# Block sums accumulated in PSUM, and the modulation product in rows of 512 with other intervals, in a two-layer diffusion backbone on one core

## The chip, the cores and the metric

The kernel runs on one core of a Trainium2 chip, as one launch. The metric is device time in microseconds (us). The engines are named as in the profile: PE (TensorE, matmuls), PEld (its weight loads), DVE (VectorE), ACT (ScalarE), POOL (GpSimd) and SP (which here only issues DMAs). Each engine works through its own list of instructions in order; semaphores hold an instruction back until what it needs is there.

## The reference, cut to what matters

The trunk has two layers over 256 context and 512 latent tokens of 1024 channels. Each layer is a half-step FFN, a token mixer (attention and gating in layer 0, a recurrence in layer 1) and a second half-step FFN. Every one of these steps is modulated by vectors that come from a product of the conditioning vector with `ada_w`:

```
mx = split(silu(c)     @ ada_w[l] + ada_b[l], 9)      # latent tokens
mc = split(silu(c_ctx) @ ada_w[l] + ada_b[l], 9)      # context tokens
h  = rmsnorm(x, g) * (1 + scale) + shift
x  = x + 0.5 * gate * ((silu(h @ wg) * (h @ wu)) @ wd) # 1024 -> 2816 -> 1024
```

Everything is float32.

## The kernel before, in words

A float32 product is made of three passes in the PE's fast format: `mm3` (lines 118 to 123) multiplies high part by high part, high by low and low by high. ACT makes the high part of an operand by a rounding copy, DVE the low part by a subtraction (`split`, line 125).

Three of the four FFNs, (layer 0, first), (layer 0, second) and (layer 1, first), save matmuls: the pairs of gate or up columns after the first pair go through `seven` (line 747), which makes a product of 2 by 2 blocks out of seven block products instead of eight. A call covers 256 columns of weights and both halves L and R (384 tokens each) of the activations; a block product is 12 matmuls of 384 columns, so a call is 84. `seven` runs 20 times per FFN, 60 times in all; it is called once for the gate (its results go to a SiLU on ACT) and once for the up weights (its results are multiplied with the SiLU by DVE and split for the down product). I call the block products M1 to M7 by their keys. Before the change they run in the order 7, 1, 6, 5, 2, 4, 3 into four PSUM banks; M2 is added to M1's bank, M4 to M7's and M3 to M5's. The remaining sums are made on DVE with an intermediate `u` = M6 - M1, which ACT starts by copying M1 out of PSUM (lines 763 to 778). The combined weight blocks for the seven products are prepared by the class `Seven` (line 202): per call four sums and seven low parts on DVE, seven high parts on ACT.

An FFN goes through groups of four column pairs' halves: four calls of `seven` (336 matmuls), then a down stage of 192 matmuls whose results ACT scales and POOL adds to a copy of x in device memory by an accumulating DMA (`down`, lines 673 to 686).

PSUM has eight banks. Before the change all of them are one pool, handed out in turn by `bank` (line 105).

The modulation (`ada_jobs`, lines 460 to 503) streams `ada_w` through SBUF in 128 chunks of 512 KB with two buffers. DVE multiplies each row of a chunk with the conditioning value of its partition and adds it up (lines 485 and 487), and per four row blocks transposes and reduces the result. This is background work: a counter of planned PE time (`clk`) runs `ada_event` (line 512), which issues one step, an instruction or two, every 500 or 800 ns of that planned time; `mod(l, m)` (line 518) issues all that is left of a vector at once when it is needed. It pauses at the end of each FFN until the next norm is done, and in the mixer of layer 0. The framework's scheduler then sets the final order of each engine's list from these issues.

Of the kernel before, what the change touches and what calls it, by code (L numbers as in the profile page):

```python
# [12 lines left out]
F32 = mybir.dt.float32  # L13
# [76 lines left out]
def hybrid_kernel(ctx: ExitStack, tc: tile.TileContext, a: dict, out: bass.AP):  # L90
# [9 lines left out]
    tp = ctx.enter_context(tc.tile_pool(name="tp", bufs=8))  # L100
    psp = ctx.enter_context(tc.tile_pool(name="psp", bufs=8, space=PSUM))
    dp = ctx.enter_context(tc.tile_pool(name="dp", bufs=1, space=DRAM))


    def bank(name="ps"):
        return psp.tile([128, 512], F32, tag="ps", name=name)

# [94 lines left out]
    class Seven(Chunk):  # L202
# [5 lines left out]
        def prep(self):  # L208
# [14 lines left out]
            before = None  # L223
            for key in (7, 1, 6, 5, 2, 4, 3):
# [183 lines left out]
    for i in range(3, 6):  # L408
# [6 lines left out]

    ada_halves = [(j, h) for j in [(0, m, cc) for m in (2, 4, 3, 5, 7, 6, 8) for cc in range(4)]
                  + [(1, m, cc) for m in (1, 0, 2, 4, 3, 5, 7, 6, 8) for cc in range(4)] for h in range(2)]
    ada_tiles, ada_seen = {}, set()

    def ada_load(i):  # L420
        if i < len(ada_halves) and i not in ada_seen:
            (l, m, cc), h = ada_halves[i]
            w = adap.tile([128, 4, 256], F32, tag="aw", name="aw")
            sp.dma_start(out=w, in_=a["ada_w"][l, h * 512:h * 512 + 512, m * 1024 + cc * 256:m * 1024 + cc * 256 + 256]
                         .rearrange("(k p) c -> p k c", p=128))
            ada_tiles[i] = w
            ada_seen.add(i)
# [32 lines left out]
    def ada_jobs():  # L460
# [14 lines left out]
        for i, ((l, m, cc), h) in enumerate(ada_halves):  # L475
# [3 lines left out]
            if h == 0:  # L479
                acc = adap.tile([128, 2, 256], F32, tag="acc", name="acc")  # L480
            for k in range(4):
                for v in range(nv):
                    s = cs[:, h * 4 + k, v:v + 1]
                    if h == 0 and k == 0:
                        dve.tensor_scalar(acc[:, v, :], w[:, k, :], s, None, op0=ALU.mult)
                    else:
                        dve.scalar_tensor_tensor(acc[:, v, :], w[:, k, :], s, acc[:, v, :], op0=ALU.mult, op1=ALU.add)  # L487
                    yield
                if k == 3 and late:
                    late.pop(0)()  # L490
            if h == 1:
                if cc == 0:
                    red = adap.tile([128, 4, nv, 8], F32, tag=f"red{nv}", name="red", bufs=1)
                t = adap.tile([128, 512], F32, tag="acc", name="acc_t")[:, 0:nv * 256]
                dve.transpose(t, acc[:, 0:nv].rearrange("p v c -> p (v c)"))
                yield
                dve.tensor_reduce(red[:, cc], t.rearrange("p (v j r) -> p v j r", v=nv, r=32), axis=mybir.AxisListType.X, op=ALU.add)
                yield
                if cc == 3:
                    late.append(lambda l=l, m=m, nv=nv, red=red: finish(l, m, nv, red))  # L500
# [4 lines left out]
    ada = ada_jobs()  # L505
    bg = {"on": True, "hold": False, "over": False}

# [132 lines left out]
    def ffn(l, j, halves, before, nxt, reserve=(), pre={}):  # L640
# [7 lines left out]
        with tc.tile_pool(name=f"ffn{l}{j}", bufs=4) as fp:  # L648
# [88 lines left out]
            def operand(key, k):  # L737
# [7 lines left out]
                return hi[kk][:, c], lo[kk][:, c]  # L745

            def seven(ch, emit):

                ps = {n: bank("pgu")[:, 0:384] for n in (7, 1, 6, 5)}
                u, v, w = (temp("uvw")[:, 0:384] for _ in range(3))  # L750
                for key, to in ((7, 7), (1, 1), (6, 6), (5, 5), (2, 1), (4, 7), (3, 5)):
                    need(ch, key)
# [6 lines left out]
                    for k in range(4):  # L759
                        mm3(ps[to], (h[:, k], lw[:, k]), operand(key, k), k == 0 and key == to, k == 3, again=key != to)  # L760
                    stream["used"] -= 1
                    pump()
                    if key == 1:
                        act.copy(u, ps[1])
                    elif key == 6:
                        dve.tensor_tensor(u, ps[6], u, op=ALU.subtract)
                        dve.tensor_tensor(v, ps[7], u, op=ALU.add)  # L767
                    elif key == 5:
                        dve.tensor_tensor(v, v, ps[5], op=ALU.subtract)
                        emit(1, R, v)  # L770
                    elif key == 2:
                        emit(0, L, ps[1])
                    elif key == 4:
                        dve.tensor_tensor(w, ps[7], u, op=ALU.add)
                        emit(1, L, w)
                    elif key == 3:
                        dve.tensor_tensor(u, ps[5], u, op=ALU.subtract)
                        emit(0, R, u)

            def gate_up_seven(p, G):  # L780
                s = {}

                def gate(f, c, src):
                    t = s[f, c.start] = temp("silu")[:, 0:384] if (f, c) == (0, L) else src
                    act.activation(t, src, AF.Silu)
# [12 lines left out]
            for gi, (f0, ng, dn) in enumerate(steps):  # L798
                G = {f: (fp.tile([128, NT], F32R, tag="ghi", name="ghi"), fp.tile([128, NT], F32R, tag="glo", name="glo"))
                     for f in range(f0, f0 + ng)}  # L800
                if gi < len(steps) - 1:
                    for p in range(f0, f0 + ng, 2):
                        if saving and p:
                            gate_up_seven(p, G)
                            continue
# [9 lines left out]
                if saving:  # L815
                    gate_up_seven(f0, G)
                    gate_up_seven(f0 + 2, G)
                    for i in range(2):
                        X[i] = xp.tile([128, 4, NT], F32, tag="x", name=f"x{i}")
# [605 lines left out]
    for cc in range(4):  # L1425
# [4 lines left out]
        if cc == 0:  # L1430
            two = arrive(*TB)
            for key in pre:
                pre[key] = bank("pre")
        for k in ks:
# [19 lines left out]
    norms = ffn(0, 0, halves, [], norm_of(0, 1), {"ahead": 1}, pre)  # L1454
    bg.update(on=True, hold=True)
    even_mixer(norms)
    norms = project_out(cwo0, halves, gates(0, 5, 1.0), norm_of(0, 2))
    bg["hold"] = False
    norms = ffn(0, 1, halves, norms, norm_of(1, 0))
# [82 lines left out]
```

## Time and profile before

| | us |
|---|---|
| median of 3 runs | 2670.96 (2668.26 to 2675.2) |
| the profiled execution | 2671.05 |
| its span | 2669.3 |
| PE busy | 2554.3 (96%) |
| PEld busy | 2367.2 (89%) |
| DVE busy | 2023.6 (76%) |
| ACT busy | 1197.1 (45%) |

The profile is one execution. Matmuls are pipelined, so a busy PE is not a PE at its full rate: the number of matmuls in a stretch tells more than the busy time. Times in the rows are microseconds from the start of the span. In this profile the first FFN lies between about 60 and 640 us, the mixer of layer 0 until about 950, the second FFN until about 1490, the third until about 2040; then come the recurrence and the last FFN, which the change does not touch.

### The profile page before, as it was taken

Reading aid. Unit: us, or ns where it says so; the run is one execution under the profiler, and the core shown is the slowest. Engines: PE = TensorE matmul, PEld = TensorE weight load, DVE = VectorE, ACT = ScalarE, POOL = GpSimd, SP = SyncE. Lnnn points to the kernel's source line nnn. Section 1 sums busy time; section 2 is a strip of 40 time slices with the busy share of each in tenths; the row PEclk is TensorE's granted clock in tenths of the full one; section 3 lists DMA queues with packets and bytes.
Section 4 is the critical chain, followed back from the end, with each engine's and each line's share of the span. In section 5 each row is a group of like instructions: output and inputs, shape, how many; then the busy total and the mean of one; then the engine's idle time right before and its main releaser. Section 6 shows DMA issues by size and latency. Waiting matters only on the chain.

```text
span 2669.3 us, 38325 instructions
## 1 busy us (share of the span) xinstructions
PE 2554.3 (96%) x14340; PEld 2367.2 (89%) x14340; DVE 2023.6 (76%) x4252; ACT 1197.1 (45%) x2325; POOL 240.8 (9%) x389
## 2 busy tenths in 40 slices
PE   7799999999999999999999998999999999999998
PEld 4689999898899998999989898999899988888887
DVE  7989989898757699999978887557467898644444
ACT  3344434444655344443444443344444997433322
POOL 0021121200000002112120010210210000000000
PEclk9899999999999999999999898999999999999999
DMA  9275575763110417556675255553553213233221
GB/s 318 64 181 139 151 170 144 183 179 122 32 33 11 149 63 175 137 154 164 163 187 185 92 142 150 96 116 91 112 128 122 64 60 114 82 102 101 95 95 56
DMA packets 281202, 328.49 MB, mean 123 GB/s; under 512 B 19984, under 2 KB 238264, under 8 KB 280504
## 3 DMA queue, kind: packets, MB, share of 16 engines
q1 hardware_dynamic: 246032, 278.69, 32.9%
q0 software_dynamic: 34560, 47.20, 11.6%
q8 instruction: 112, 1.84, 0.3%
q14 instruction: 74, 0.61, 0.1%
q10 hardware_dynamic: 424, 0.15, 0.0%
HBM read 262.04 MB, written 63.96 MB: 122 GB/s over the span
## 4 chain that ended last, share of the span: by engine, by line
PE 70%; DVE 17%; DMA 5%; ACT 4%; issue 2%; POOL 1%; SPq 0%; ACTq 0%; DVEq 0%; POOLq 0%
PE pgu L112 33%; PE pd L112 20%; PE ps L112 9%; PE po L112 4%; DMA aw<-in_ada_w_dram 4%; DVE acc L487 4%; DVE w L219 3%; PE pv L112 1%; DVE w L192 1%; PE sl L112 1%; PE pt L1080 1%; PE sc L112 1%; DVE hlo L598 1%; ACT w L189 1%; DVE glo L127 1%
## 5 line engine op out<-in xcount | busy, mean ns | idle before, releaser
L112 PE MATMUL pgu<-hhi,w 128*128 128x384 f32 (+2 forms) x3008 | 830.3, 350 | 33.7 <-DVE uvw L767 14.7
L112 PE MATMUL pd<-ghi,w 128*128 128x256 f32 (+2 forms) x2528 | 651.6, 345 | 9.4 <-ACT ghi L126 9.2
L112 PEld LDWEIGHTS pgu<-hhi,w 128*128 128x128 f32 x3008 | 556.7, 191 | 65.6 <-DVE uvw L767 17.1
L112 PE MATMUL pgu<-hlo,w 128*128 128x384 f32 (+2 forms) x1504 | 524.4, 349 | 1.9 <-DVE hlo L598 1.4
L112 PEld LDWEIGHTS pd<-ghi,w 128*128 128x128 f32 x2528 | 444.7, 190 | 63.3 <-ACT ghi L126 13.8
L112 PE MATMUL pd<-glo,w 128*128 128x512 f32 (+2 forms) x1264 | 435.0, 346 | 1.9 <-DVE glo L127 1.9
L112 PE MATMUL pgu<-form,w 128*128 128x384 f32 x2160 | 405.0, 338 | 9.1 <-ACT form L126 6.8
L112 PEld LDWEIGHTS pgu<-form,w 128*128 128x128 f32 x2160 | 379.7, 189 | 14.1 <-ACT form L126 7.4
L487 DVE SCALAR_TENSOR_TENSOR acc<-aw,cs,acc 128x256 f32<-128x256 f32 x784 | 343.9, 481 | 38.2 <-DMA aw<-in_ada_w_dram 36.5
L189 ACT ACTIVATE w<-raw 128x512 fp32r<-128x512 f32 x396 | 241.0, 627 | 202.6 <-PE pgu L112 79.9
L192 DVE TENSOR_TENSOR w<-raw,w 128x512 fp32r<-128x512 f32 x396 | 267.8, 688 | 76.3 <-ACT w L189 74.1
L684 POOL DMA_DIRECT2D kept<-add x240 | 208.9, 948 | 1188.7 <-ACT add L683 1176.3
L219 DVE TENSOR_TENSOR w<-raw,w 128x512 fp32r<-128x512 f32 x360 | 239.5, 686 | 94.4 <-ACT w L236 93.8
L112 PEld LDWEIGHTS pgu<-hlo,w 128*128 128x128 f32 x1504 | 288.1, 192 | 15.9 <-DVE hlo L598 2.3
L236 ACT ACTIVATE w<-raw 128x512 fp32r<-128x512 f32 x360 | 213.9, 625 | 185.4 <-DVE raw L233 89.3
L112 PEld LDWEIGHTS pd<-glo,w 128*128 128x128 f32 x1264 | 240.8, 191 | 29.9 <-DVE glo L127 5.3
L683 ACT ACTIVATE add<-pd,gate 128x256 f32<-128x256 f32 x240 | 136.9, 579 | 202.4 <-PE pd L112 177.7
L112 PE MATMUL ps<-hhi,w 128*128 128x384 f32 (+1 forms) x704 | 197.6, 355 | 4.8 <-ACT t L1296 3.4
L112 PEld LDWEIGHTS ps<-hhi,w 128*128 128x128 f32 x704 | 132.5, 194 | 11.8 <-ACT t L1296 4.1
L112 PE MATMUL ps<-hlo,w 128*128 128x384 f32 (+1 forms) x352 | 124.7, 354 | 3.3 <-DVE hlo L598 3.2
L112 PE MATMUL po<-hhi,w 128*128 128x384 f32 (+1 forms) x512 | 114.3, 313 | 2.5 <-ACT hhi L126 2.5
L637 DVE SCALAR_TENSOR_TENSOR x<-pd,gate,x 128x256 f32<-128x256 f32 (+3 forms) x128 | 69.9, 564 | 52.6 <-PE pd L112 51.9
(293 smaller groups left out, 3072.5 us busy)
## 6 DMA issues: line engine op xcount, KB each, us to landing
aw<-in_ada_w_dram SPq DMA_DIRECT2D x128, 512.0 KB, 5.2
raw<-in_ffn_w_gate_dram SPq DMA_DIRECT2D x44, 1024.0 KB, 5.5
raw<-in_ffn_w_up_dram SPq DMA_DIRECT2D x44, 1024.0 KB, 5.5
raw<-in_ffn_w_down_dram SPq DMA_DIRECT2D x40, 1024.0 KB, 5.1
kept<-add POOLq DMA_DIRECT2D x120, 256.0 KB, 5.8
kept<-add POOLq DMA_DIRECT2D x120, 128.0 KB, 5.9
x<-kept SPq DMA_DIRECT2D x48, 192.0 KB, 4.1
fw<-in_ada_w_dram SPq DMA_DIRECT2D x16, 512.0 KB, 9.1
```

Source lines behind the costliest of these rows:

```text
L112: pe.matmul(o, w, x, start=start, stop=stop, skip_group_check=again)
L127: dve.tensor_tensor(lo, src, hi.bitcast(F32), op=ALU.subtract)
L189: act.activation(tiles[i][:, 0:512], self.raw[:, i * 512:i * 512 + 512], AF.Copy)
L192: dve.tensor_tensor(t[:, 512:1024], self.raw[:, i * 512 - 512:i * 512], t[:, 0:512].bitcast(F32), op=ALU.subtract)
L219: dve.tensor_tensor(l, src[key], h.bitcast(F32), op=ALU.subtract)
L236: act.activation(halves_of(key)[0], src[key], AF.Copy)
L487: dve.scalar_tensor_tensor(acc[:, v, :], w[:, k, :], s, acc[:, v, :], op0=ALU.mult, op1=ALU.add)
L598: dve.scalar_tensor_tensor(H[1][k][:, s:e], h[:, o], self.B[:, k, v:v + 1], H[0][k][:, s:e].bitcast(F32), op0=ALU.add, op1=ALU.subtract)
L637: dve.scalar_tensor_tensor(x, ps[:, s - c0:e - c0], g[:, d, v:v + 1], x, op0=ALU.mult, op1=ALU.add)
L683: act.activation(t, ps[:, 0:c1 - c0], AF.Copy, scale=state["gate"][:, 4 * c + d, v:v + 1])
L684: pool.dma_start(out=saved(l, j)[:, 4 * c + d, c0:c1], in_=t, accum_op=ALU.add)
L1080: pe.transpose(ps[:, o:o + 128], self.src[hh][b + bb], ident)
```

## The change

Two parts.

The sums. Two of the eight banks (a pool `psx` of two, beside `psp` with six) are held through the stretch of `seven` calls of an FFN, one for M6 and one for M5. One matmul each (`hold`) writes them first, so that later matmuls, which do not start a sum there, add to what the bank holds. In a call M1 and M7 come first, in banks of their own. ACT writes -M1 into M6's bank and M6 is added to it by PE; ACT writes the negative of that sum into M5's bank and M5 is added to that. M4 is then added to M6's bank and M3 to M5's. With that DVE has two sums per call left (five before), ACT two writes into PSUM more. The order of the products becomes 1, 7, 6, 2, 5, 4, 3, and `Seven` prepares them in that order. While the two banks are held all other work rotates through six banks (`banks["six"]`).

The modulation. A chunk is 128 x 2 x 512 instead of 128 x 4 x 256: the same 512 KB in rows of 2 KB instead of 1 KB, and half as many DVE instructions of twice the length. A step is issued every 800 ns of planned time until the first gate vector is there, then every 2000 (first FFN), 6000 and 2500 ns (later).

```diff
-    psp = ctx.enter_context(tc.tile_pool(name="psp", bufs=8, space=PSUM))
+    psp = ctx.enter_context(tc.tile_pool(name="psp", bufs=6, space=PSUM))
+    psx = ctx.enter_context(tc.tile_pool(name="psx", bufs=2, space=PSUM))
...
-            w = adap.tile([128, 4, 256], F32, tag="aw", name="aw")
+            w = adap.tile([128, 2, 512], F32, tag="aw", name="aw")
...
-            for k in range(4):
+            for k in range(2):
                 for v in range(nv):
-                    s = cs[:, h * 4 + k, v:v + 1]
+                    s = cs[:, h * 2 + k, v:v + 1]
...
-            clk.at(500.0 if mods_done.get((0, 2), 0) < 4 else 800.0, ada_event)
+            clk.at(800.0 if mods_done.get((0, 2), 0) < 4 else bg["every"], ada_event)
...
+            def hold():
+                banks["six"] = True
+                for n in (6, 5):
+                    held[n] = psx.tile([128, 512], F32, tag="px", name="seeded")[:, 0:384]
+                    mm(held[n], hi[0][:, 0:128], hi[0][:, L], True, True)
...
-                for key, to in ((7, 7), (1, 1), (6, 6), (5, 5), (2, 1), (4, 7), (3, 5)):
+                for key, to in ((1, 1), (7, 7), (6, 6), (2, 1), (5, 5), (4, 6), (3, 5)):
...
                     if key == 1:
-                        act.copy(u, ps[1])
+                        act.activation(ps[6], ps[1], AF.Copy, scale=-1.0)
                     elif key == 6:
-                        dve.tensor_tensor(u, ps[6], u, op=ALU.subtract)
-                        dve.tensor_tensor(v, ps[7], u, op=ALU.add)
-                    elif key == 5:
-                        dve.tensor_tensor(v, v, ps[5], op=ALU.subtract)
-                        emit(1, R, v)
+                        act.activation(ps[5], ps[6], AF.Copy, scale=-1.0)
+                    elif key == 7:
+                        act.copy(u, ps[7])
                     elif key == 2:
                         emit(0, L, ps[1])
+                    elif key == 5:
+                        dve.tensor_tensor(v, u, ps[5], op=ALU.subtract)
+                        emit(1, R, v)
                     elif key == 4:
-                        dve.tensor_tensor(w, ps[7], u, op=ALU.add)
-                        emit(1, L, w)
+                        dve.tensor_tensor(u, u, ps[6], op=ALU.add)
+                        emit(1, L, u)
                     elif key == 3:
-                        dve.tensor_tensor(u, ps[5], u, op=ALU.subtract)
-                        emit(0, R, u)
+                        emit(0, R, ps[5])
```

How the lists move is seen best at three places. First, ACT's list in the fifth call of `seven`, a gate call (`raw` is loaded weights, `w` prepared ones, `silu` and `uvw` or `uv` temporaries); before:

```order
L764 COPY uvw<-pgu 128x384
L236 ACTIVATE w<-raw 128x512 x4
L785 ACTIVATE uvw<-uvw 128x384
L785 ACTIVATE silu<-pgu 128x384
L236 ACTIVATE w<-raw 128x512
```

and after, where `seeded` is a held bank:

```order
L784 ACTIVATE seeded<-pgu 128x384
L788 COPY uv<-pgu 128x384
L245 ACTIVATE w<-raw 128x512 x3
L786 ACTIVATE seeded<-seeded 128x384
L245 ACTIVATE w<-raw 128x512 x2
L805 ACTIVATE silu<-pgu 128x384
```

One read of PSUM has become three, the two writes to held banks stand among the weight copies, and a product of the PE waits for each of them.

Second, DVE's list in the third down stage of the second FFN (`acc` is the modulation's sum, `aw` a chunk of `ada_w`); before:

```order
L485 TENSOR_SCALAR acc<-aw,cs 128x256
L219 TENSOR_TENSOR w<-raw,w 128x512 x2
L485 TENSOR_SCALAR acc<-aw,cs 128x256
L487 SCALAR_TENSOR_TENSOR acc<-aw,cs,acc 128x256 x14
L495 STREAM_TRANSPOSE acc_t<-acc 128x512
L485 TENSOR_SCALAR acc<-aw,cs 128x256 x2
L487 SCALAR_TENSOR_TENSOR acc<-aw,cs,acc 128x256 x6
L219 TENSOR_TENSOR w<-raw,w 128x512 x2
L235 TENSOR_TENSOR raw<-raw 128x4x128
L487 SCALAR_TENSOR_TENSOR acc<-aw,cs,acc 128x256 x2
L219 TENSOR_TENSOR w<-raw,w 128x512
L487 SCALAR_TENSOR_TENSOR acc<-aw,cs,acc 128x256 x6
```

and after:

```order
L496 SCALAR_TENSOR_TENSOR acc<-aw,cs,acc 128x512 x2
L228 TENSOR_TENSOR w<-raw,w 128x512 x2
L496 SCALAR_TENSOR_TENSOR acc<-aw,cs,acc 128x512
L244 TENSOR_TENSOR raw<-raw 128x4x128
L496 SCALAR_TENSOR_TENSOR acc<-aw,cs,acc 128x512 x8
L228 TENSOR_TENSOR w<-raw,w 128x512
L496 SCALAR_TENSOR_TENSOR acc<-aw,cs,acc 128x512
L228 TENSOR_TENSOR w<-raw,w 128x512 x3
L237 TENSOR_TENSOR s_12035<-raw 128x512
```

The 32 scalar products and additions shown of before, out of 38 in the whole stage, have become 12 out of 14, and the next call's weight sum (the last row) follows at once.

Third, DVE's list late in the second down stage of the first FFN, where the next call's first weight sum (`s_2502`, and `s_2409` after) and its low part fall; before:

```order
L487 SCALAR_TENSOR_TENSOR acc<-aw,cs,acc 128x256 x10
L228 TENSOR_TENSOR s_2502<-raw 128x512
L487 SCALAR_TENSOR_TENSOR acc<-aw,cs,acc 128x256
L230 TENSOR_TENSOR raw<-raw 128x4x128
L219 TENSOR_TENSOR w<-s_2502,w 128x512
L495 STREAM_TRANSPOSE acc_t<-acc 128x512
L497 TENSOR_REDUCE red<-acc_t 128x16
L485 TENSOR_SCALAR acc<-aw,cs 128x256 x2
L487 SCALAR_TENSOR_TENSOR acc<-aw,cs,acc 128x256 x14
L219 TENSOR_TENSOR w<-raw,w 128x512
```

and after:

```order
L506 TENSOR_REDUCE red<-acc_t 128x2x8
L494 TENSOR_SCALAR acc<-aw,cs 128x512 x2
L496 SCALAR_TENSOR_TENSOR acc<-aw,cs,acc 128x512 x14
L479 TENSOR_TENSOR mods_153<-ps,veca 32x16 x4
L237 TENSOR_TENSOR s_2409<-raw 128x512
```

The 16 products and additions in a row, two chunks before, are four chunks now, each with a load of its own; and the weight sum that stood ahead of them stands behind them.

## Rows read from the trace of the kernel before

**Rows 1.** The page's busy time by engine: us, share of the span, instructions.
```profile
PE 2554.3 (96%) x14340; PEld 2367.2 (89%) x14340; DVE 2023.6 (76%) x4252; ACT 1197.1 (45%) x2325; POOL 240.8 (9%) x389
```
**Rows 2.** The chain that ended last, shares of the span by line.
```profile
by line: PE pgu L112 33.0%; PE pd L112 19.6%; PE ps L112 8.8%; PE po L112 3.9%; DMA aw<-in_ada_w_dram 3.5%; DVE acc L487 3.5%; DVE w L219 2.6%; issue 2.4%; PE pv L112 1.4%; DVE w L192 1.0%; PE sl L112 1.0%; PE pt L1080 0.8%; PE sc L112 0.8%
```
**Rows 3.** By stretch: length, busy us and count of each engine, clock, DMA share, GB/s.
```profile
60.00:200.00 140.00, 119.75 (x607) 105.92 (x606) 132.99 (x301) 52.34 (x103) 14.08 (x16) 0.90 0.45 123
200.00:660.00 460.00, 446.16 (x2494) 426.36 (x2493) 416.77 (x901) 192.28 (x363) 61.77 (x88) 0.97 0.59 157
960.00:1460.00 500.00, 486.12 (x2738) 460.63 (x2737) 450.22 (x944) 214.25 (x396) 69.57 (x80) 0.99 0.59 153
1460.00:1520.00 60.00, 53.33 (x270) 50.91 (x269) 48.29 (x120) 22.40 (x47) 6.66 (x24) 0.89 0.43 141
1520.00:1660.00 140.00, 129.81 (x716) 123.00 (x715) 121.78 (x258) 57.27 (x111) 14.00 (x16) 0.95 0.47 125
1660.00:1900.00 240.00, 240.00 (x1374) 226.38 (x1374) 130.04 (x221) 101.90 (x188) 41.56 (x48) 1.00 0.51 107
```
**Rows 4.** DVE instructions by line and form: count, busy us, mean ns, idle before.
```profile
L487 DVE SCALAR_TENSOR_TENSOR acc<-aw,cs,acc 128x256 f32<-128x256 f32 x784 | 343.9, 481 | 38.2 <-DMA aw<-in_ada_w_dram 36.5
...
L766 DVE TENSOR_TENSOR uvw<-pgu,uvw 128x384 f32<-128x384 f32 x60 | 33.2, 554 | 10.6 <-PE pgu L112 9.7 <-issue 0.6
...
L637 DVE SCALAR_TENSOR_TENSOR x<-pd,gate,x 128x512 f32<-128x512 f32 x40 | 29.9, 749 | 39.3 <-PE pd L112 39.3
```
**Rows 5.** The same view of ACT.
```profile
L785 ACT ACTIVATE uvw<-uvw 128x384 f32<-128x384 f32 x90 | 46.9, 522 | 97.3 <-issue 32.4 <-DVE uvw L769 31.1 <-DVE uvw L774 18.6
...
L764 ACT COPY uvw<-pgu 128x384 f32<-128x384 f32 x60 | 28.3, 471 | 49.1 <-PE pgu L112 37.7 <-issue 10.2 <-ACT w L236 1.2
```
**Rows 6.** Waits: us in total, times, longest.
```profile
ACT add L683 <- PE pd L112: 177.7, 140, 2.8
...
DVE acc L487 <- DMA aw<-in_ada_w_dram: 36.5, 17, 7.7
DVE acc L485 <- DMA aw<-in_ada_w_dram: 33.5, 14, 4.8
```
**Rows 7.** Timeline, PE: two products together (6 and 5) of three calls.
```profile
305.30 4.32 PE L112 MATMUL pgu<-form,w 128*128 128x384 f32 x24
...
1087.36 4.32 PE L112 MATMUL pgu<-form,w 128*128 128x384 f32 x24
...
1758.84 4.32 PE L112 MATMUL pgu<-form,w 128*128 128x384 f32 x24
```
**Rows 8.** Timeline, ACT and DVE: who reads them, and when.
```profile
310.50 0.52 DVE L769 TENSOR_TENSOR uvw<-uvw,pgu 128x384 f32<-128x384 f32 x1
...
1087.55 0.48 ACT L764 COPY uvw<-pgu 128x384 f32<-128x384 f32 x1
...
1093.42 0.56 DVE L769 TENSOR_TENSOR uvw<-uvw,pgu 128x384 f32<-128x384 f32 x1
...
1763.20 0.56 DVE L769 TENSOR_TENSOR uvw<-uvw,pgu 128x384 f32<-128x384 f32 x1 [0.20 <-PE pgu L112]
```
**Rows 9.** Timeline, DVE at a chunk, and PE's waits in two calls.
```profile
378.86 3.26 DVE L487 SCALAR_TENSOR_TENSOR acc<-aw,cs,acc 128x256 f32<-128x256 f32 x8 [7.75 <-DMA aw<-in_ada_w_dram]
...
391.50 0.57 PE L112 MATMUL pgu<-hhi,w 128*128 128x384 f32 x1 [1.85 <-DVE uvw L767]
...
1621.94 0.69 PE L112 MATMUL pgu<-hhi,w 128*128 128x384 f32 x1 [8.40 <-ACT uvw L764]
```
**Rows 10.** DMA issues: engine, count, KB each, median us from issue to landing.
```profile
aw<-in_ada_w_dram SPq DMA_DIRECT2D x128, 512.0 KB, 5.2
raw<-in_ffn_w_gate_dram SPq DMA_DIRECT2D x44, 1024.0 KB, 5.5
...
raw<-in_ffn_w_down_dram SPq DMA_DIRECT2D x40, 1024.0 KB, 5.1
```

More of the change, by code (lines that the diff above doesn't have):

```diff
@@ L100, in hybrid_kernel @@
     tp = ctx.enter_context(tc.tile_pool(name="tp", bufs=8))
-    psp = ctx.enter_context(tc.tile_pool(name="psp", bufs=8, space=PSUM))
+    psp = ctx.enter_context(tc.tile_pool(name="psp", bufs=6, space=PSUM))
+    psx = ctx.enter_context(tc.tile_pool(name="psx", bufs=2, space=PSUM))
     dp = ctx.enter_context(tc.tile_pool(name="dp", bufs=1, space=DRAM))
+    banks = {"n": 0, "six": False}
     def bank(name="ps"):
+        banks["n"] = (banks["n"] + 1) % 8
+        if banks["n"] >= 6 and banks["six"]:
+            banks["n"] = 0
+        if banks["n"] >= 6:
+            return psx.tile([128, 512], F32, tag="px", name=name)
         return psp.tile([128, 512], F32, tag="ps", name=name)
@@ L223, in prep @@
             before = None
-            for key in (7, 1, 6, 5, 2, 4, 3):
+            for key in (1, 7, 6, 2, 5, 4, 3):
                 stream["used"] += 1
@@ L414, in hybrid_kernel @@
     stream["ahead"] = 0
-    ada_halves = [(j, h) for j in [(0, m, cc) for m in (2, 4, 3, 5, 7, 6, 8) for cc in range(4)]
-                  + [(1, m, cc) for m in (1, 0, 2, 4, 3, 5, 7, 6, 8) for cc in range(4)] for h in range(2)]
+    ada_halves = [(j, h) for j in [(0, m, cc) for m in (2, 4, 3, 5, 7, 6, 8) for cc in range(2)]
+                  + [(1, m, cc) for m in (1, 0, 2, 4, 3, 5, 7, 6, 8) for cc in range(2)] for h in range(4)]
     ada_tiles, ada_seen = {}, set()
@@ L488, in ada_jobs @@
                     yield
-                if k == 3 and late:
-                    late.pop(0)()
-            if h == 1:
+            if late:
+                late.pop(0)()
+            if h == 3:
                 if cc == 0:
                     red = adap.tile([128, 4, nv, 8], F32, tag=f"red{nv}", name="red", bufs=1)
[L494 to L499, printed above, removed]
+                for v in range(nv):
+                    t = temp("acc_t")
+                    dve.transpose(t, acc[:, v])
+                    dve.tensor_reduce(red[:, 2 * cc:2 * cc + 2, v], t.rearrange("p (c j r) -> p c j r", c=2, r=32), axis=mybir.AxisListType.X, op=ALU.add)
+                    yield
+                if cc == 1:
                     late.append(lambda l=l, m=m, nv=nv, red=red: finish(l, m, nv, red))
@@ L505, in hybrid_kernel @@
     ada = ada_jobs()
-    bg = {"on": True, "hold": False, "over": False}
+    bg = {"on": True, "hold": False, "over": False, "every": 2000.0}
     def ada_step():
@@ L745, in operand @@
                 return hi[kk][:, c], lo[kk][:, c]
+            held = {}
+            def hold():
[3 more added lines that the diff above has]
+                    mm(held[n], hi[0][:, 0:128], hi[0][:, L], True, True)
             def seven(ch, emit):
-                ps = {n: bank("pgu")[:, 0:384] for n in (7, 1, 6, 5)}
-                u, v, w = (temp("uvw")[:, 0:384] for _ in range(3))
-                for key, to in ((7, 7), (1, 1), (6, 6), (5, 5), (2, 1), (4, 7), (3, 5)):
+                ps = {n: bank("pgu")[:, 0:384] for n in (1, 7)}
+                ps.update(held)
+                u, v = (temp("uv")[:, 0:384] for _ in range(2))
+                for key, to in ((1, 1), (7, 7), (6, 6), (2, 1), (5, 5), (4, 6), (3, 5)):
                     need(ch, key)
@@ L759, in seven @@
                     for k in range(4):
-                        mm3(ps[to], (h[:, k], lw[:, k]), operand(key, k), k == 0 and key == to, k == 3, again=key != to)
+                        w, x = (h[:, k], lw[:, k]), operand(key, k)
+                        mm3(ps[to], w, x, k == 0 and key in (1, 7), k == 3, again=key not in (1, 7))
                     stream["used"] -= 1
@@ L783, in gate @@
                 def gate(f, c, src):
-                    t = s[f, c.start] = temp("silu")[:, 0:384] if (f, c) == (0, L) else src
+                    t = s[f, c.start] = src if f else temp("silu")[:, 0:384]
                     act.activation(t, src, AF.Silu)
@@ L803, in ffn @@
                         if saving and p:
+                            if not held:
+                                hold()
                             gate_up_seven(p, G)
@@ L817, in ffn @@
                     gate_up_seven(f0 + 2, G)
+                    banks.update(six=False, n=5)
                     for i in range(2):
@@ L1431, in hybrid_kernel @@
             two = arrive(*TB)
-            for key in pre:
-                pre[key] = bank("pre")
+            for i, key in enumerate(pre):
+                pre[key] = bank("pre") if i < 2 else psx.tile([128, 512], F32, tag="px", name="pre")
+            banks["six"] = True
         for k in ks:
@@ L1454, in hybrid_kernel @@
     norms = ffn(0, 0, halves, [], norm_of(0, 1), {"ahead": 1}, pre)
-    bg.update(on=True, hold=True)
+    bg.update(on=True, hold=True, every=6000.0)
     even_mixer(norms)
     norms = project_out(cwo0, halves, gates(0, 5, 1.0), norm_of(0, 2))
-    bg["hold"] = False
+    bg.update(hold=False, every=2500.0)
     norms = ffn(0, 1, halves, norms, norm_of(1, 0))
```

4 lines of the change are left out of this document (2 added, 2 removed).

## The prediction, made before the changed kernel was run

> **What bounds the kernel now.** I read the page first, then the chain, then stretches of time, then single waits. The page gives PE as busy nearly throughout, DVE at 76% and ACT at 45% [rows 1]. The chain runs mostly through the PE's matmuls, but 7% of it is the modulation: 3.5% loads of its chunks, 3.5% its additions on DVE; weight preparation on DVE adds 2.6% and 1.0% [rows 2]. So the bound is PE, with DVE in its way at places. Where, the stretches tell [rows 3]. From 1660 to 1900 us the modulation is over, DVE is busy 130 of 240 us, and the PE makes 1374 matmuls: 240 / 1374 = 0.1747 us each, its full rate on this mix. I hold the other stretches against that rate:
>
> - 60 to 200 us: 607 x 0.1747 = 106.0, so 34.0 us lost (start; the mix is another one, so this is rough).
> - 200 to 660, first FFN: 2494 gives 435.6, 24.4 lost; DVE busy 417 of 460.
> - 960 to 1460, second FFN: 2738 gives 478.3, 21.7 lost; DVE busy 450 of 500.
> - 1460 to 1520, from the second FFN to the third: 270 gives 47.2, 12.8 lost.
> - 1520 to 1660, third FFN while the modulation lasts: 716 gives 125.1, 14.9 lost; DVE busy 122 of 140.
>
> That is 107.8 us; 73.8 without the start. Nothing else that the change touches can be won. The losses come in pieces: a chunk comes late, DVE stands still with all that is behind it in its list (7.75 us until 378.86), and some 12 us later the PE waits for DVE's sums (until 391.50); until 1621.94 it waits 8.40 us for ACT's copy of M1 [rows 9]. DVE's waits for chunks are 36.5 + 33.5 = 70.0 us in 31 pieces [rows 6].
>
> **What the change removes on DVE.** Sums: three per call, 60 calls, 0.554 us [rows 4]: 180 x 0.554 = 99.7 us. Modulation: 784 additions of 256 at 0.481 us, 377 us, become 392 of 512. The trace has this operation at 512 columns with another source at 0.749 us [rows 4], so 294 us, 83 less. The scalar products halve too, and transposes and reductions go from 64 to 56 of each; I count these as nothing. Together some 183 us by mean duration. These overlap a little back to back (784 x 0.481 is 377 against 344 busy), so I take 165 us. None of it is on the PE's path as such: it counts only where DVE is late. In the three stretches of the FFNs about 150 of DVE's 989 busy us go, and its share falls from 90% of 1100 us to about 76%, near what it has where the PE never waits (54%, from 1660 on).
>
> **What it adds.** Three seed matmuls, half a microsecond: nothing. 120 writes of ACT into PSUM. The trace has no such write; the nearest rows are ACT's copy out of PSUM, 0.471 us, and its SiLU from SBUF, 0.522 us [rows 5]. I take 0.47, so 56 us on an engine that is idle for half the time; between nothing (each within its cover) and 31 us (all 60 calls late by half a microsecond) in the end.
>
> The waits matter more than the durations. Within a call three products now wait for a short chain: M6 for ACT's write after M1, M5 for ACT's write after M6, M3 for DVE's read of M5's bank. Each has one product between as cover: 12 x 0.1747 = 2.10 us. Before, the reads of a bank that a later product adds to had two or more products. With 0.47 to 0.56 us for the operation, ACT or DVE may begin 1.5 us late before the PE stops; then everything behind on the PE's list, the whole call and the down stage, stops with it. How late they are, three calls show. Around 305 M5 ends at 309.62 [rows 7] and DVE reads at 310.50 [rows 8]: 0.88 late. Around 1087, in the second FFN, M5 ends at 1091.68 and DVE reads at 1093.42: 1.74 late, over the limit by 0.2. Around 1759, without modulation, M5 ends at 1763.16 and DVE reads at 1763.20. ACT reads M1 at 1087.55, 0.04 after the matmuls' recorded end at 1087.51 (the next two products begin at 1087.36 and overlap the last by 0.15). The worst of these lags belongs to a DVE at 90%; at 76% I expect that of the first FFN or less. I charge 4 us for the calls that still come late: 20 waits of 0.2 us.
>
> **The modulation's chunks.** The bytes stay, so each chunk still takes about 5.2 us to land, two buffers [rows 10]. A chunk was eight DVE instructions, now four: in a run one lasts 4 x 0.749 = 3.0 us instead of 8 x 0.481 = 3.8, so a run of chunks waits more for each; but runs become rarer. In the second FFN's third down stage 14 products and additions stand where 38 stood, 3.5 chunks instead of almost five, and the next weights follow behind them without a rival. In the first FFN a run of four chunks stands where two stood, ahead of the next weight sum: one wait of before could well remain there, or grow.
>
> The Trainium skill, Perfetto Trace Analysis, section DMA Optimizations, says that small transfers, under 2 KB, carry a considerable overhead each; the rows of a chunk go from 1 KB to 2 KB. In this trace loads of 1 MB with rows of 1 KB land in 5.5 us and with rows of 2 KB in 5.1 [rows 10], so the effect is there and small: by it a chunk would gain some 0.2 us, 128 chunks a few us where one is waited for.
>
> **The sum.** Start: DVE's work up to the first down products falls by a few of 130 us, 3 of 34.0 us recovered. First FFN: 9 of 24.4 (the run of four chunks keeps the rest). Second FFN: 16 of 21.7, three quarters, as DVE's list has emptied there. Transition: 4 of 12.8; its list now has no chunk in the last down stage, but the chain of the norm stays. Third FFN: 3 of 14.9; its last chunks, with half the arithmetic per byte, still come close together. Late calls: -4. Sum 3 + 9 + 16 + 4 + 3 - 4 = 31 us. From the profiled execution, 2671.05 (1.75 over its span, and 0.1 from the median 2670.96), that is 2640 us. If everything but half the start were recovered, 73.8 + 17 = 91, it would be 2580; 2602 needs three quarters of that.
>
> **The rivals.** A, the chunks are the bound, not DVE's load: the waits for loads stay, as bytes and buffers do, and the runs of four chunks make them as long as before. For it: 70 us of waits [rows 6] and the waits of PE that follow them [rows 9]. Against it: DVE waits for a chunk only where its list wants one faster than every 5.2 us, which the longer intervals avoid in most stages. Then only a third of the second FFN's 21.7 is won, 7, less 4 for late calls: 2668.
>
> B, the coupling: the PE now walks in step with ACT and DVE, three times per call. If DVE's lag stays at 1.74 us and ACT's list, which waits for DVE's weight sums in order, lags as much, each wait costs up to 0.2 us beyond the cover and a late chunk hits the PE at once instead of after two calls' slack. At 0.2 for all three waits of the 40 calls beside modulation that is 24 us, and with nothing recovered the time is 2695. It decides from a lag of 1.5 us on. Against it: the lag of 0.88 in the first FFN, under the limit at 91% load already.
>
> C, the banks: with two held, all else rotates through six. The Trainium skill, Perfetto Trace Analysis, section Matmul Optimizations, asks for all eight PSUM banks to be in use, which speaks against the change. Here a down product of 2.1 us may keep its bank for five more products, 10 us, and ACT's reads are waiting for the PE, not the PE for them (177.7 us, at most 2.8 at a time [rows 6]). So by the trace it costs nothing; by the rule some 120 down products late by 0.2 us would eat 24 of the 31 us, 2664.
>
> **How the numbers follow.** My forecast, DVE relieved and most waits gone: 0.71. A: 0.13, B: 0.12, C: 0.04. What a measurement can tell from no change is about 0.3%, 8 us: 2663 to 2679. Faster than that: the forecast, 0.71. Within: A and C with some of B's mild form, 0.16. Slower: the rest of B, 0.13. The range goes from 2602 (most of the losses gone) to 2677, where A and C still lie inside and only B is outside; the forecast's own range is 2602 to 2663.
>
> **What would show it.** Right: DVE's busy time near 1860 us; from 960 to 1460 us the full rate in nearly all calls; no wait of the PE for `seeded` beyond some us in sum; waits for chunks well under 70 us. Wrong: PE waits for L784, L786 or L792 at tens of microseconds (B); waits for chunks as before, with the PE's stops at the starts of calls (A); PE waits for L692's reads of down products (C).

## The result and the profile after

| | us |
|---|---|
| before, median of 4 runs | 2671.59 (2668.26 to 2675.2) |
| after, median of 4 runs | 2635.70 (2634.55 to 2638.63) |
| ratio | 0.9867, 95% interval 0.985 to 0.9884 |
| predicted | 2640 (2602 to 2677) |
| profiled execution after, its span | 2636.69, 2634.9 |

The kernel is 36 us faster, four from the forecast. The sections below show that the time came out right while one of its reasons did not, so that the close match is in part luck.

The page of the changed kernel: busy time by engine, and the chain that ended last by line.

```profile
PE 2538.1 (96%) x14346; PEld 2354.7 (89%) x14346; DVE 1880.2 (71%) x3608; ACT 1255.9 (48%) x2445; POOL 240.4 (9%) x389
...
PE pgu L121 16%; PE pd L121 12%; PE ps L121 9%; PE seeded L121 8%; POOL kept L693 4%; PE po L121 3%; PE pv L121 1%; DVE acc L496 1%; DMA aw<-in_ada_w_dram 1%; DMA kept<-add 1%; PE sl L121 1%; PE sc L121 1%; PE pt L1103 1%; DVE w L201 1%; DVE w L228 1%
```

DVE has 143 us less to do, ACT 59 us more; the modulation's loads and additions have shrunk on the chain from 3.5% each [rows 2] to 1% each (26% of the new chain is `issue`, time for which the profile shows no wait, so the two chains compare only roughly).

By stretch, after (columns as in [rows 3]):

```profile
200.00:660.00 460.00, 449.68 (x2548) 428.46 (x2547) 370.51 (x683) 215.93 (x416) 62.58 (x88) 0.99 0.60 157
960.00:1460.00 500.00, 496.51 (x2841) 474.35 (x2840) 385.38 (x691) 238.46 (x449) 71.83 (x92) 1.00 0.58 148
```

At 0.1747 us per matmul the first stretch now loses 460 - 2548 x 0.1747 = 14.9 us (24.4 before) and the second 3.7 (21.7 before). Since the two kernels are at different work at the same time, I also compare the start of the last matmul of the same down stage in both traces (the differences are taken before rounding):

| up to the end of | before | after | after minus before |
|---|---|---|---|
| the first down stage | 182.8 | 186.7 | +3.9 |
| the first FFN | 623.6 | 614.9 | -8.6 |
| the second FFN's first down stage | 1051.9 | 1042.7 | -9.2 |
| its fourth | 1333.8 | 1320.1 | -13.8 |
| the second FFN | 1495.8 | 1462.8 | -33.0 |
| the third FFN's first down stage | 1604.8 | 1578.1 | -26.7 |
| the third FFN | 2039.5 | 2002.9 | -36.6 |
| the program's last matmul | 2658.7 | 2624.3 | -34.4 |

More than half, 19 us, is won in the last two stages of the second FFN, where DVE waited seven times for a chunk before, 15 us in all; 6 us of it is lost for a while at the third FFN's start.

Not all that is won is time in which the PE stood still. Span less PE busy falls from 115.0 to 96.8 us, which is 18.2 of the 34.4 us between the two spans; the other 16.2 us are PE busy time, for six matmuls more. The clock that TensorE was granted has its part in that. In before, around the longest stop of the PE (from 1613.54 to 1621.94 us, [rows 9]), columns as in [rows 3]:

```profile
1600.00:1613.50 13.50, 13.50 (x78) 12.55 (x76) 6.07 (x14) 3.72 (x7) 4.40 (x5) 1.00 1.06 242
1617.00:1630.60 13.60, 7.75 (x23) 7.25 (x24) 13.21 (x31) 4.09 (x8) 0.00 (x0) 0.50 0.49 155
```

Ahead of the stop the clock is 1.00 (2.4 GHz) and a matmul takes 0.17 us; from 1617.0 to 1630.6, while the PE stands still and after it, the clock is 0.50 (1.2 GHz) and a matmul takes 0.34. This stop thus cost more than its own length. Over the whole span the mean granted clock is 0.976 before and 0.984 after: 2669.3 x 0.024 = 64 us and 2634.9 x 0.016 = 42 us of full clock not granted. The 22 us between them are my estimate, from above, of the clock's share in the 36 us, as the PE stands still in a part of the slow stretches.

Single operations, DVE and ACT, by line and form (columns as in [rows 4, 5]):

```profile
L496 DVE SCALAR_TENSOR_TENSOR acc<-aw,cs,acc 128x512 f32<-128x512 f32 x392 | 283.4, 748 | 40.6 <-DMA aw<-in_ada_w_dram 40.0
...
L786 ACT ACTIVATE seeded<-seeded 128x384 f32<-128x384 f32 x60 | 28.5, 475 | 47.5 <-PE seeded L121 47.2
L784 ACT ACTIVATE seeded<-pgu 128x384 f32<-128x384 f32 x60 | 28.5, 475 | 39.7 <-PE pgu L121 39.5
```

An addition of 512 takes 748 ns (749 taken), a write into PSUM 475 ns (470 taken). The waits after (total, times, longest):

```profile
ACT add L692 <- PE pd L121: 226.8, 172, 2.5
...
DVE acc L496 <- DMA aw<-in_ada_w_dram: 40.0, 19, 5.2
...
DVE acc L494 <- DMA aw<-in_ada_w_dram: 7.5, 1, 7.5
...
PE seeded L121 <- ACT seeded L784: 5.4, 5, 2.3
...
PE seeded L121 <- ACT seeded L786: 1.3, 2, 0.7
PE seeded L121 <- DVE uv L792: 1.1, 2, 0.8
```

DVE waits for chunks 47.5 us (70.0 before, [rows 6]); the PE waits for the three new couplings 7.8 us in all. The timeline of one call in the second FFN shows why so little (PE's rows are the products 7 and 6):

```profile
1074.61 0.47 ACT L784 ACTIVATE seeded<-pgu 128x384 f32<-128x384 f32 x1 [0.47 <-PE pgu L121]
...
1074.41 2.28 PE L121 MATMUL pgu<-form,w 128*128 128x384 f32 x12
1076.52 2.25 PE L121 MATMUL seeded<-form,w 128*128 128x384 f32 x12
```

ACT is done at 1075.08 and M6 begins at 1076.52: 1.44 us to spare. Over the 60 calls the median to spare is 1.44 us for M6 in each of the three FFNs and 1.35 for M5, and 1.20 to 1.33 for M3, which waits for DVE.

### The profile page after: what moved, and what is told of

Same layout as the page of the kernel before. It is cut to its first block, busy times and chain, and to the rows that moved or that the text cites. A ratio compares the mean times of both kernels' runs of the same rounds, so it can differ in the third digit from the quotient of the medians.

```text
span 2634.9 us, 37738 instructions
## 1 busy us (share of the span) xinstructions
PE 2538.1 (96%) x14346; PEld 2354.7 (89%) x14346; DVE 1880.2 (71%) x3608; ACT 1255.9 (48%) x2445; POOL 240.4 (9%) x389
## 4 chain that ended last, share of the span: by engine, by line
PE 53%; issue 26%; DVE 8%; POOL 5%; ACT 4%; DMA 3%; SPq 0%; POOLq 0%; ACTq 0%; DVEq 0%
PE pgu L121 16%; PE pd L121 12%; PE ps L121 9%; PE seeded L121 8%; POOL kept L693 4%; PE po L121 3%; PE pv L121 1%; DVE acc L496 1%; DMA aw<-in_ada_w_dram 1%; DMA kept<-add 1%; PE sl L121 1%; PE sc L121 1%; PE pt L1103 1%; DVE w L201 1%; DVE w L228 1%
## 5 line engine op out<-in xcount | busy, mean ns | idle before, releaser
L121 PE MATMUL pgu<-hhi,w 128*128 128x384 f32 (+2 forms) x2048 | 572.0, 351 | 2.1 <-ACT w L245 0.8
L121 PE MATMUL pd<-glo,w 128*128 128x256 f32 (+2 forms) x1264 | 431.8, 342 | 0.6 <-DVE glo L136 0.6
L121 PEld LDWEIGHTS pgu<-hhi,w 128*128 128x128 f32 x2048 | 375.5, 189 | 29.9 <-ACT hhi L601 1.5
L121 PE MATMUL pgu<-hlo,w 128*128 128x384 f32 (+2 forms) x1024 | 358.8, 351 | 1.3 <-DVE hlo L607 1.2
L496 DVE SCALAR_TENSOR_TENSOR acc<-aw,cs,acc 128x512 f32<-128x512 f32 x392 | 283.4, 748 | 40.6 <-DMA aw<-in_ada_w_dram 40.0
L121 PE MATMUL seeded<-form,w 128*128 128x384 f32 x1440 | 275.1, 338 | 15.5 <-ACT form L135 6.7
L121 PEld LDWEIGHTS seeded<-form,w 128*128 128x128 f32 x1440 | 252.4, 189 | 20.6 <-ACT seeded L784 7.7
L121 PE MATMUL seeded<-hhi,w 128*128 128x384 f32 x960 | 258.9, 339 | 7.8 <-ACT hhi L135 6.7
L121 PEld LDWEIGHTS seeded<-hhi,w 128*128 128x128 f32 x960 | 176.8, 190 | 9.8 <-ACT hhi L135 7.6
L121 PE MATMUL seeded<-hlo,w 128*128 128x384 f32 x480 | 161.8, 338 | 0.0
```

The lines of the kernel that those rows point to most:

```text
L121: pe.matmul(o, w, x, start=start, stop=stop, skip_group_check=again)
```

## The experiments

Two theories. **Load**: DVE's list is shorter, and each part of the change counts by what it takes off DVE (this is the prediction's forecast). **Chunks**: what costs time is DVE standing still before a chunk that has not landed, with the next call's weights queued behind it (the prediction's rival A without its conclusion); what counts is when chunks are wanted. Beside them the rivals B (coupling) and C (banks).

### The parts one by one

Three parts: the sums (with their banks), rows of 512, and the pace (the intervals).

Sums alone: the change with these parts put back:

```diff
-            w = adap.tile([128, 2, 512], F32, tag="aw", name="aw")
+            w = adap.tile([128, 4, 256], F32, tag="aw", name="aw")
...
-            clk.at(800.0 if mods_done.get((0, 2), 0) < 4 else bg["every"], ada_event)
+            clk.at(500.0 if mods_done.get((0, 2), 0) < 4 else 800.0, ada_event)
```

> The sums of the change alone; the modulation as before (rows of 256, 500 and 800 ns). Load theory (DVE has less to do, each part counts by its share of the 165 us taken off DVE): DVE busy 2023.6 - 85, about 1940 us, and some 18 of the 36 us: 2653 us. Chunk theory (what counts is when chunks are wanted and land): DVE's waits for chunks stay at 70 us or grow, as DVE comes to them earlier, the PE's stops after them stay: 2664 to 2672. Coupling theory (three PSUM waits per call, 1.35 us of slack each, only with an even modulation): a late chunk hits the PE at once, waits of the PE for L784, L786 and L792 of 10 us or more in sum, 2675 or more.

The change with the old pace (twice the old interval, as a step now does twice the columns):

```diff
-            clk.at(800.0 if mods_done.get((0, 2), 0) < 4 else bg["every"], ada_event)
+            clk.at(1000.0 if mods_done.get((0, 2), 0) < 4 else 1600.0, ada_event)
```

> The change with the old pace of the modulation: rows of 512, a step every 1000 and then 1600 ns, which is the old number of bytes per planned time. Load theory: DVE's work is that of the change, so its time: 2636 to 2640. Chunk theory: the pace was the point; the time falls back toward before, 2655 to 2665, with waits for chunks above the 47.5 us of the change.

Before with rows of 512 alone, at the old pace:

```diff
-            w = adap.tile([128, 4, 256], F32, tag="aw", name="aw")
+            w = adap.tile([128, 2, 512], F32, tag="aw", name="aw")
...
-            clk.at(500.0 if mods_done.get((0, 2), 0) < 4 else 800.0, ada_event)
+            clk.at(1000.0 if mods_done.get((0, 2), 0) < 4 else 1600.0, ada_event)
```

> Before with rows of 512 alone, at the old pace in bytes (1000 and 1600 ns); sums on DVE and eight banks as before. Load theory: DVE busy 2023.6 - 70, about 1950 us, and some 15 us won: 2656. Chunk theory: a chunk's arithmetic is shorter while its load is not, so DVE waits more for chunks: 2665 to 2675.

The same with the change's pace:

```diff
-            clk.at(1000.0 if mods_done.get((0, 2), 0) < 4 else 1600.0, ada_event)
+            clk.at(800.0 if mods_done.get((0, 2), 0) < 4 else bg["every"], ada_event)
```

> The modulation of the change alone (rows of 512 and its intervals), sums on DVE and eight banks as before. Load theory: as rows of 512 alone, 2656. Chunk theory: most of the gain, 2640 to 2648, DVE's waits for chunks below 50 us.

Before with rows of 256 at the change's pace:

```diff
-            clk.at(500.0 if mods_done.get((0, 2), 0) < 4 else 800.0, ada_event)
+            clk.at(400.0 if mods_done.get((0, 2), 0) < 4 else bg["every"], ada_event)
```

> Before with rows of 256 at the change's pace in bytes (a step every 400, then 1000, 3000 and 1250 ns), sums on DVE and eight banks as before. If the pace spreads the chunks and that is what counts: 2655 to 2660, DVE's waits for chunks below 50 us. If the rows of 512 are needed for it (a column block is summed over four chunks instead of two, so there are fewer transposes and fewer instructions): 2668 to 2674, waits for chunks near 70 us.

| kernel | us | ratio to before, interval | DVE busy | DVE's waits for chunks |
|---|---|---|---|---|
| before | 2671 to 2674 | 1 | 2023.6 | 70.0 |
| sums | 2668.33 | 0.9985, 0.9971 to 1.0 | 1943.0 | 59.9 |
| rows | 2656.52 | 0.9948, 0.9927 to 0.9968 | 1960.7 | 36.6 |
| pace | 2654.85 | 0.9934, 0.9917 to 0.995 | 2024.5 | 52.2 |
| sums and rows | 2642.02 | 0.9897, 0.987 to 0.9924 | 1882.7 | 30.5 |
| rows and pace | 2640.93 | 0.9883, 0.9857 to 0.9909 | 1961.3 | 38.1 |
| all three | 2635.70 | 0.9867, 0.985 to 0.9884 | 1880.2 | 47.5 |

The pace alone takes nothing off DVE and wins 18 us. The sums alone take 81 us off DVE, the most of any part, and win 3 us (0 to 8 by the interval). So what a part takes off DVE does not tell what it wins, and the load theory fails for these two.

The chunk theory has misses too. It had the times of the sums alone and of rows with pace right (the waits of the sums alone not: 59.9 us, where 70 or more was expected), and the pace alone just at the edge (2654.85, with waits of 52.2 us where below 50 was expected). But rows alone came out at the load theory's time (2656), not at 2665 to 2675, and sums and rows (2642.02) near the load theory's 2636 to 2640, not at 2655 to 2665; in both the waits were shorter than it had them (36.6 us against more than 70, 30.5 against more than 47.5). Rows of 512 and the pace together win 31 us without the sums. The sums on top of rows at the old pace are worth 14.5 us; on top of both they are worth 5, where the two intervals overlap. What the 14.5 us are I did not find: no run tells a shorter list on DVE from chunks that are asked for at other times. The sum of the waits does not order the times either (47.5 us is the fastest kernel of the table), so where a wait falls seems to matter. With rows alone, one wait of 6.9 us at 1050 us, at the second FFN's start, is among those that undo 9 of the 10 us won in the first FFN; sums and rows together have 1.2 us there.

How a chunk reaches the PE, in before at the longest stop of all [rows 9]:

```profile
1611.29 2.04 DVE L487 SCALAR_TENSOR_TENSOR acc<-aw,cs,acc 128x256 f32<-128x256 f32 x4 [7.22 <-DMA aw<-in_ada_w_dram]
...
1618.62 0.68 DVE L233 TENSOR_TENSOR raw<-raw 128x512 f32<-128x512 f32 x1
...
1619.34 2.19 ACT L236 ACTIVATE w<-raw 128x512 fp32r<-128x512 f32 x4 [13.40 <-DVE raw L233]
1621.43 0.46 ACT L764 COPY uvw<-pgu 128x384 f32<-128x384 f32 x1
```

DVE waits 7.22 us for a chunk; the weight sum L233 stands behind it; ACT's copy of that sum waits 13.40 us; and ACT's read of M1, ready long ago, stands behind that copy. With the sums alone the same place is worse:

```profile
1606.80 2.05 DVE L496 SCALAR_TENSOR_TENSOR acc<-aw,cs,acc 128x256 f32<-128x256 f32 x4 [11.25 <-DMA aw<-in_ada_w_dram]
...
1616.93 0.63 ACT L245 ACTIVATE w<-s 128x512 fp32r<-128x512 f32 x1 [14.09 <-DVE s L237]
1617.46 0.47 ACT L784 ACTIVATE seeded<-pgu 128x384 f32<-128x384 f32 x1
...
1617.99 4.21 PE L121 MATMUL seeded<-form,w 128*128 128x384 f32 x12 [11.71 <-ACT seeded L784]
```

The new write L784 stands in the same position as the old read did; the PE stops 11.71 us. Its 12 matmuls then take 4.21 us, where those at 1076.52 above took 2.25. So at this place DVE's sums were not the link that held the PE; ACT's list behind a weight sum behind a chunk was, and the change keeps that link. After has it once more, at 1579 us, shorter:

```profile
1579.46 0.48 DVE L494 TENSOR_SCALAR acc<-aw,cs 128x512 f32<-128x512 f32 x1 [7.53 <-DMA aw<-in_ada_w_dram]
...
1583.91 0.63 ACT L245 ACTIVATE w<-s 128x512 fp32r<-128x512 f32 x1 [4.66 <-DVE s L237]
1584.44 0.47 ACT L784 ACTIVATE seeded<-pgu 128x384 f32<-128x384 f32 x1
...
1584.97 3.69 PE L121 MATMUL seeded<-form,w 128*128 128x384 f32 x12 [2.29 <-ACT seeded L784]
```

### No loads

Both kernels with all but two chunk loads left out; the additions read the same two tiles again and again, so the modulation vectors are not the reference's. The edit (of the change; that of before is the same with its tile):

```diff
+            if i > 1:
+                ada_tiles[i] = ada_fixed[i % 2]
+                ada_seen.add(i)
+                return
             w = adap.tile([128, 2, 512], F32, tag="aw", name="aw")
+            ada_fixed.append(w)
```

> Before with the loads of the modulation's chunks left out after the first two: all products and additions read those two tiles (the modulation vectors are wrong by that). DVE's list is the same, it never waits for a chunk. Chunk theory: the PE's stops after late chunks go, 25 to 35 us won: 2637 to 2647. Load theory: the 70 us of waiting go, but the 896 instructions stay and DVE at 76% still comes late: at most half, 2655 to 2665.

> The change with the loads of its chunks left out after the first two (the modulation vectors are wrong by that). Before without its loads took 2620.9. If DVE's shorter list is worth anything by itself, this kernel, with 140 us less on DVE than that one, is clearly below: 2600 to 2612. If only waits for chunks cost time: 2617 to 2624, the same as before without loads, though DVE does less; then some 15 us of the change are still lost to chunks.

Measured: before without loads 2620.90 (0.9804, 0.9782 to 0.9826), after without loads 2618.85 (0.9798, 0.9777 to 0.9818). Their pages:

```profile
PE 2534.6 (97%) x14340; PEld 2354.7 (90%) x14340; DVE 2026.2 (77%) x4252; ACT 1202.2 (46%) x2325; POOL 242.1 (9%) x389
```
```profile
PE 2535.6 (97%) x14346; PEld 2357.8 (90%) x14346; DVE 1880.9 (72%) x3608; ACT 1256.3 (48%) x2445; POOL 240.9 (9%) x389
```

This is the sharpest of the experiments. Without waits for chunks 145 us less on DVE are worth 2 us, which is no more than the medians scatter. (That is net of the couplings' own cost: in the trace of after without loads the PE waits 2.2 us for ACT's two writes.) To the old kernel, with DVE's list unchanged, leaving the loads out is worth 51 us, more than the chunk theory's 25 to 35. 66 MB of traffic go with the loads, so 51 us is a bound from above for the waits; but ACT and DVE wait for weight loads nearly as long without the chunk loads as with them (27 us against 30), so little of it can come from weights that land late. Of the 53 us from before to after without loads the change won 36 and left 17.

### Banks and coupling

Before with two banks held through the calls and not used:

```diff
+                            if not held:
+                                hold()
                             gate_up_seven(p, G)
...
+                    banks.update(six=False, n=5)
```

> Before with the change's six banks: two banks are held through the seven calls and not used, the sums stay on DVE. Rival C (the banks bind): each call's four banks and the down products share six, PE waits for reads of banks, 10 us or more: 2682 or more. If the banks are free of cost: 2669 to 2674.

Measured 2673.51, ratio 0.9997 (0.9983 to 1.001): eight banks or six, no difference. Rival C falls.

The change with each write into a held bank made four or six times:

```diff
-                        act.activation(ps[6], ps[1], AF.Copy, scale=-1.0)
+                        for _ in range(4):
+                            act.activation(ps[6], ps[1], AF.Copy, scale=-1.0)
...
-                        act.activation(ps[5], ps[6], AF.Copy, scale=-1.0)
+                        for _ in range(4):
+                            act.activation(ps[5], ps[6], AF.Copy, scale=-1.0)
```

> The change with each of ACT's two writes into a held bank made four times over (the same values): three more of about 0.39 us back to back, so the product that waits loses 1.2 us of its 1.35 to 1.44 us of slack. If the slack is what the trace shows: no change but for the calls that are late already, 2636 to 2642, and DVE and PE wait little more. Coupling theory in its strict form (any lengthening of the chain is paid): 120 x 1.2 = 140 us more.

> As before it with six writes: five more, 2.0 us on a slack of 1.35 to 1.44. If the slack is the cover: each of the 120 products waits 0.55 to 0.65 us, 66 to 78 us more, 2702 to 2715, in waits of the PE for L786 and L784. If the PE could take other work meanwhile, nothing.

Measured 2680.55 and 2724.13, 45 and 88 us over the change. Four writes should have been free by my expectation, and were not; six were expected at 2702 to 2715 and cost more. ACT's timeline with four writes:

```profile
1805.48 0.98 ACT L785 ACTIVATE seeded<-pgu 128x384 f32<-128x384 f32 x2 [0.83 <-PE pgu L121]
1806.38 0.62 ACT L245 ACTIVATE w<-raw 128x512 fp32r<-128x512 f32 x1
1806.90 0.48 ACT L785 ACTIVATE seeded<-pgu 128x384 f32<-128x384 f32 x1
1807.31 0.62 ACT L245 ACTIVATE w<-raw 128x512 fp32r<-128x512 f32 x1
1807.83 0.48 ACT L785 ACTIVATE seeded<-pgu 128x384 f32<-128x384 f32 x1
```

The four are not back to back: weight copies stand between them, and from the first's start to the last's end it is 2.42 us (median of the 60) where the cover is one product, 2.10 us. 0.32 us x 120 is 38 of the 45. With six it is 4.0 us, 1.9 beyond the cover, yet 88 / 120 = 0.73 us are paid: in its list the next product and part of the down stage then stand ahead of the waiting product. So the coupling is real, its edge lies near the end of the cover, not all that goes beyond it is paid, and the change stands 1.35 to 1.44 us inside it.

### Smaller chunks

The change with chunks of half the size in four buffers, and then with a slower pace in the third FFN:

```diff
-            w = adap.tile([128, 2, 512], F32, tag="aw", name="aw")
+            w = adap.tile([128, 512], F32, tag="aw", name="aw", bufs=4)
...
-            ada_load(i + 1)
+            ada_load(i + 3)
...
+    bg["every"] = 4000.0
     norms = ffn(1, 0, halves, norms, norm_of(1, 1))
```

> The change with chunks of 256 KB (one row block of 512 columns) in four buffers instead of 512 KB in two: the same SBUF, the same arithmetic in the same order, a load goes out after half a chunk's work. Chunk theory: a load has one and a half chunks of DVE work to land in instead of one, so DVE's waits for chunks fall from 47 to 15 to 25 us, and 5 to 10 us are won: 2626 to 2631. Load theory: DVE's work is the same, so is the time: 2634 to 2638. If the doubled number of issues on SP costs (128 more of 0.37 us, in line with the weight loads): 2640 or more.

> Chunks of 256 KB in four buffers, and the modulation in the third FFN at a step every 4000 ns instead of 2500 (its last 64 instructions then spread over the whole FFN, where DVE is half idle, instead of its first third, where the next activations are combined on DVE too). With the chunks of 256 KB alone 14 of 22 us of DVE's waits lie between 1557 and 1687 us and the calls there still lose time. Chunk theory: those waits halve and the third FFN's first calls gain 3 to 6 us: 2623 to 2627. If the loss there is the combining of activations and not the chunks: 2628 to 2631.

Measured 2629.20 (0.9836, 0.982 to 0.9853) and 2624.91 (0.9825, 0.98 to 0.9851), each inside the chunk theory's range. The waits and the loads with half chunks:

```profile
DVE acc L494 <- DMA aw<-in_ada_w_dram: 21.9, 15, 6.9
```
```profile
aw<-in_ada_w_dram SPq DMA_DIRECT2D x256, 256.0 KB, 4.1
```

With the slower third FFN:

```profile
DVE acc L494 <- DMA aw<-in_ada_w_dram: 29.8, 22, 5.7
```

DVE's work is unchanged, the waits fall from 47.5 to 21.9 us and 6.5 us are won. The calls between the third FFN's first and second down stage take 59.7 us then, not 64.3 as in the change. With the slower pace as well they take 58.9, so that pace gains 0.8 us there and not the 3 to 6 that I expected, and the waits sum to more again, 29.8 us. Its trace ends 5.0 us earlier than that of half chunks alone; 3.1 of them lie between the end of the second FFN and the third's first down stage. So the second time is in the range for a reason that the run does not show. This version beats both kernels, by 47 and 11 us. The size of a chunk and the number of buffers change together here, so these runs do not tell which of the two shortens the waits.

The Trainium skill, Perfetto Trace Analysis, section DMA Optimizations, says that splitting DMAs into smaller chunks may let some start sooner; this case agrees, with DVE's waits down from 47.5 to 21.9 us. Its other rule there, that transfers under 2 KB pay an overhead, is about a whole transfer, and the prediction used it for the rows of a chunk; for these no run here shows a steady effect: chunks with rows of 1 KB landed in 5.2 us (before), 5.0 (sums alone) and 4.9 (pace alone), with rows of 2 KB in 4.9 (rows alone), 5.3 (sums and rows), 5.5 (rows and pace) and 4.6 (after).

## Why the prediction was right, and where not

- **The sum**: 31 us forecast, 36 measured. By stage: start -3 forecast, +3.9 measured; first FFN -9 against -12.5; second -16 against -24.4 (0.6 of it up to its first down stage); transition, third FFN and late calls together -3 against -3.6. In the recurrence 2.2 us were lost that I did not expect. I did not look for the cause of the start's loss; rows and pace without the sums show 0.9 us there. The sum agrees in part by luck: the start went the other way, and the second FFN won half as much again as forecast. I counted the losses by matmuls against the full rate and called them waits; they also held the stretches at the lower clock.
- **What the change removes on DVE**: 165 us forecast, 143 measured, and the step from there to the PE failed. I let the sums and the modulation count alike, through DVE's share of time. The sums are 81 us of it and win 3 us alone; without waits for chunks DVE's whole relief is worth 2. DVE's 90% in a stretch was no bound, though it looked like one. What remains open is the 14.5 us that the sums win on top of rows at the old pace.
- **Rival A** had the right place and the wrong conclusion. The chunks were the bound, but its sentence that waits stay as bytes and buffers do was wrong: with the bytes and the buffers of before, rows alone took the waits from 70.0 to 36.6 us and the pace alone to 52.2. My own rows held this: 70 us in 31 pieces [rows 6] and the longest stop of the PE behind such pieces [rows 9], and I gave it 0.13. The chances of the time bands did not add either: A and C alone are 0.17, not 0.16 with a part of B, and what is left of B's 0.12 cannot be 0.13.
- **The cover of 2.10 us** and the write at 0.47 us were right; so was the 4 us charge in size (7.8 us of waits). The lag of 1.74 us of the second FFN [rows 8] is rare now: DVE's read of M5's bank begins within 0.5 us in 53 of the 60 calls, and later than 1.74 us in four (6.4 at most).
- **Banks**: as forecast, no cost.

## What to carry to other kernels

An engine that is busy 90% of a stretch is not yet the bound: before counting what an edit takes off it, leave out the loads that it waits for and see what is left. Background work that is streamed in chunks costs by what stands behind a chunk that has not landed, through every in-order list it passes (here DVE, then ACT, then the PE); here another pace alone (18 us) and smaller chunks in the same memory (6.5 us) were worth more than the sums taken off DVE alone (3 us). A long stop of the PE can cost more than its length: after the one of 8.40 us matmuls took twice as long until the clock was back. Adding in PSUM on a value that another engine writes cost next to nothing here while the write ended inside the one product that stands between (6.7 us of waits for 120 writes), and 45 us once it took 0.3 us longer than that product.

## What the runs showed of the hardware that was not expected

A load that DVE waited for was issued as soon as its buffer was free (0.03 us after, median) and took 8.0 us to its use in before (31 loads) and 7.3 after (20 loads), where the median over the loads whose landing the trace holds (67 and 63 of 128) is 5.2 and 4.6. Slow loads are the likelier ones to be waited for, so this does not show that a load is slower because it is wanted; it shows that the median, which the prediction used, is too low a price for a wait. A load of half the size landed in 4.1 us instead of 4.6, so by these medians most of a load's time here does not go by its bytes.
